# Hybrid attention block on one core: GpSimd forms the weight sums of gates and up stage, and gates' blocks take four groups of eight by seven products

## The chip, the cores and the metric

The kernel runs on one core of a Trainium2 chip. A core has five engines that each work through a queue of their own, in order: TensorE (PE: matmuls into PSUM, with a separate unit that loads weights), VectorE (DVE), ScalarE (ACT), GpSimd (POOL) and SyncE (SP, which here issues nearly all DMAs). They meet through semaphores. Operands lie in SBUF, 128 partitions wide; sums of matmuls in eight banks of PSUM. The metric is device time in microseconds (us) from the first to the last instruction, median of several runs.

## What is computed

One layer of a hybrid block on 256 tokens of width 2048, float32 throughout (the heads' attention is left out here):

```python
h = rms_norm(x, g_mix)
proj = h @ w_in                      # heads' queries, keys, values, and 3 x 2048 gate columns
o_fox, o_sb, o_mem = ...
g = sigmoid(gates.reshape(b, s, 3, 2048) + b_gate)
merged = g[:, :, 0] * (o_fox @ w_br_fox) + g[:, :, 1] * (o_sb @ w_br_sb) + g[:, :, 2] * (o_mem @ w_br_mem)
x = x + merged @ w_out
h2 = rms_norm(x, g_ffn)
u = causal_depthwise_conv(h2 @ w_up, conv_w, conv_b)     # w_up is 2048 x 11264
u_gate, u_val = split(u, 2)
x = x + (silu(u_gate) * u_val) @ w_down                  # w_down is 5632 x 2048
```

The weights are read once, so the kernel streams them: some 390 MB pass through the DMA queues in a run.

## The kernel before

**Split products.** TensorE reads float32 operands in a rounded form, so every weight tile of 128 x 1024 (`raw`) is split in two: ScalarE copies it rounded (`hi`, L143 in `piece`, L378 in `parts`), VectorE subtracts (`lo`, L144 and L379: two SBUF operands). A product is three matmuls (L384 to L386 in `three`): the two parts of the activations with `hi`, the first with `lo`. There are four buffers each for raw, hi and lo. In the up stage the same is done with two matmuls per tile (L1318, L1319).

**Seven products for eight.** In the functions that `blocked` drives, a group of two 128-row slices of weights (a "pair") times two halves of the tokens, on two halves of 1024 columns, is eight products of 512 columns: `eight`, written "e" in a plan. By a Strassen-Winograd scheme the same pair takes seven, "s", if four sums of the weights' quarters (T1 to T4) and four of the activations' quarters (formed by `pair_sums`) are there. The sums of activations for gates are the tile `xs`, one entry per "s" of a block, made in the background by `x_sums`, `GS` of them.

Where the weight sums come from differs:
- For `w_out` and `w_down` they are formed ahead, in stages that have time for it, and stored in HBM (`kept`). `sums_in` (L252 to L256) makes them with three VectorE adds on a staged tile of 128 x 1024 `pre` or `staged`: one of half its columns with a broadcast operand, two of a quarter each, where the tile is a half (`half_sums`); with a whole pair of 2048 columns (`pair_sums_ahead`) 1024, 512 and 512 columns. Both generators are stepped by `tick`, once per weight tile: they issue the load on SP, some ticks later the adds, some ticks later the store on SP. `half_sums` runs beside gates' plain block and the branch products, one half in 8 ticks; `pair_sums_ahead` runs in the stage of heads and again in the up stage, one pair in 8 ticks, from tick `DU` = 22 on, 17 pairs there.
- Two pairs of `w_down` get their sums in HBM itself (`sums_in_hbm`, L323): a tiny GpSimd copy that waits for an activation, then eight DMAs issued by GpSimd, four of them accumulating, each waiting for the one before it. `last_sums` starts the first at tick 148 of the up stage.
- For gates (`w_in`) the sums are formed on the spot: `prepared` (L492) loads the pair's two raw tiles and forms T1, T3, T2, T4 in two block tiles `t_g` with four VectorE adds of 512 columns (L496 to L499). It is called one pair ahead, and `seven_here` then splits and multiplies.

**Stages.** Memory keys and values, x, projections of the heads with their attention beside them (until about 304 us), gates and branches (304 to 655), `w_out` (to about 738), up (to 1226), down (to the end). Gates are six blocks of 1024 columns: the first is done plainly by `product`, five by `blocked` with a plan of eight letters, here "esesesee": two in a row, branch products, then three in a row, and branch products. In a block of gates, background generators are not stepped (`go_on`).

**Order.** A planner orders each engine's queue by the cost it expects of each instruction and by what is ready; `in_order` (`keep_in_program_order`) pins an instruction behind the one that was traced before it on its engine. The adds of `sums_in`, the loads and stores of the generators and the matmuls in `three` (from gates on) are pinned, the four adds of `prepared` are not.

**GpSimd** otherwise does little: masks of 128 x 128 in the heads' attention (L952, L983) and the DMAs of a few small rearrangements.

Of the kernel before, what the change touches and what calls it, by code (L numbers as in the profile page):

```python
# [10 lines left out]
F32 = mybir.dt.float32  # L11
F32R = mybir.dt.float32r
AF = mybir.ActivationFunctionType
ALU = mybir.AluOpType
AX = mybir.AxisListType

P = 128
# [17 lines left out]
WBUFS = 4  # L35
SBUFS = 4
BLOCKS = 14
GS = 3
PF = (6, 5)
DU = 22  # L40

# [2 lines left out]
def hybrid_block(  # L44
# [25 lines left out]
    nc = tc.nc  # L70
# [154 lines left out]


    o_plans = ("eessssse", "eessssse")
    g_plans = (("", "esesesee", "esesesee"), ("esesesee", "esesesee", "esesesee"))
    d_plans = (
        "efefefef" + "sef" * 4 + "ssefsfssfssee",  # L230
        "efsss" * 3 + "efssfsssssee",
# [2 lines left out]
    T1, T3, T4, T2 = range(4)  # L234
    FS2, FS4, FS3, FS1 = range(4)
    in_order = tc.keep_in_program_order
# [12 lines left out]
        for h in range(2)  # L249
    )  # L250

    def sums_in(w):  # L252
        both = w[:, 1:2].to_broadcast([P, 2, w.shape[2]])
        in_order(nc.vector.tensor_tensor(w[:, 0:2], w[:, 0:4:3], both, ALU.add))
        in_order(nc.vector.tensor_tensor(w[:, T2], w[:, T1], w[:, T2], ALU.add))
        in_order(nc.vector.tensor_tensor(w[:, T4], w[:, T2], w[:, T4], ALU.add))  # L256

    def kept_for(name, nb, pr):
        if (name, nb, pr) not in sums_of:
            at = f"kept_{name}{nb}_{pr}"  # L260
            sums_of[name, nb, pr] = dram.tile([P, 4, 512], F32, tag=at, name=at)
        return sums_of[name, nb, pr]

    def half_sums(staging, period, add, store, end):

        while halves and end not in issued:
            name, wv, nb, pr, h = halves.popleft()
            kept = kept_for(name, nb, pr)
            w = staging(f"pre_{name}{nb}_{pr}_{h}").rearrange("p (i c) -> p i c", i=4)
            n0 = nb * PIECE + h * 256  # L270
            for n in range(2):
                in_order(
                    nc.sync.dma_start(
                        w.rearrange("p (k n) c -> p k n c", k=2)[:, :, n],
                        wv[:, 2 * pr : 2 * pr + 2, n0 + n * 512 : n0 + n * 512 + 256],
                    )
                )
            for _ in range(add):
                yield
            sums_in(w)  # L280
            for _ in range(store - add):
                yield
            in_order(nc.sync.dma_start(kept[:, :, h * 256 : (h + 1) * 256], w))
            for _ in range(period - store):
                yield

    def pair_sums_ahead(staging, period, add, store, most=99, delay=0):

        due = deque()
        clock = 0  # L290
        for _ in range(delay):
            yield

        def step():
            while due and due[0][0] <= clock:
                _, kept, w = due.popleft()
                in_order(nc.sync.dma_start(kept, w))

        periods = cycle(period if isinstance(period, tuple) else (period,))
        while len(halves) > 1 and halves[0][-1] == 0 and most:  # L300
            most -= 1
            name, wv, nb, pr, _ = halves.popleft()
            halves.popleft()
            kept = kept_for(name, nb, pr)
            w = staging(f"pre_{name}{nb}_{pr}")
            in_order(
                nc.sync.dma_start(
                    w.rearrange("p (k c) -> p k c", k=2), wv[:, 2 * pr : 2 * pr + 2, nb * PIECE : (nb + 1) * PIECE]
                )
            )  # L310
            w = w.rearrange("p (i c) -> p i c", i=4)
            due.append((clock + store, kept, w))
            for t in range(next(periods)):
                if t == add:
                    sums_in(w)
                step()
                clock += 1
                yield
        while due:
            step()  # L320
            clock += 1
            yield
# [65 lines left out]
    def pair_sums(pair, w, groups):  # L388

        v = pair.bitcast(F32).rearrange("p k (l c) -> p k l c", l=2)  # L390
        wa, wr = w if isinstance(w, tuple) else (w[:, :512], w[:, 512:])
        a, r = (half.rearrange("p (i q) -> p i q", i=4) for half in (wa, wr))
        nc.vector.tensor_tensor(wa.rearrange("p (k c) -> p k c", k=2), v[:, :, 0], v[:, :, 1], ALU.add)

        a10 = a[:, 1:2].to_broadcast([P, 2, P])
        nc.vector.tensor_tensor(r[:, FS3 : FS1 + 1], a[:, 0:4:3], a10, ALU.subtract)
        nc.vector.scalar_tensor_tensor(r[:, FS2], r[:, FS1], -1.0, a[:, 0], ALU.mult, ALU.subtract)
        nc.vector.tensor_tensor(r[:, FS4], r[:, FS2], a[:, 2], ALU.add)
        for dst, which in groups:
            nc.scalar.copy(dst[..., 0, :], r[:, which])  # L400
        for dst, which in groups:
            nc.vector.tensor_tensor(dst[..., 1, :], r[:, which], dst[..., 0, :].bitcast(F32), ALU.subtract)
# [20 lines left out]
    def blocked(name, w, nb, n0, plan, pair, sums, raw_tile, t4_tile, gathered, ready=None, form=None, apart=None):  # L423
# [14 lines left out]
        def load(k):  # L438
            raw = raw_tile(f"raw_{name}{nb}_{k}")
            nc.sync.dma_start(raw, wv[:, k, n0 : n0 + PIECE])  # L440
            return raw
# [50 lines left out]
        def prepared(p):  # L492
            raw0, raw1 = load(2 * p), load(2 * p + 1)
            t13, t42 = (t4_tile(f"t{i}_{name}{nb}_{p}") for i in range(2))
            b0, b1, u, v = (w.rearrange("p (n c) -> p n c", n=2) for w in (raw0, raw1, t13, t42))
            nc.vector.tensor_tensor(u[:, 0], b0[:, 0], b0[:, 1], ALU.add)  # L496
            nc.vector.tensor_tensor(u[:, 1], b0[:, 1], b1[:, 1], ALU.add)
            nc.vector.tensor_tensor(v[:, 1], u[:, 0], b1[:, 1], ALU.add)
            nc.vector.tensor_tensor(v[:, 0], v[:, 1], b1[:, 0], ALU.add)  # L499
            return raw0, raw1, t13, t42  # L500

        def seven_here(p, first, last):
# [20 lines left out]
        for i, c in enumerate(plan):  # L523
            if c == "s":
                if s == 0:
                    if ready:
                        ready()
                    Y += [bank(f"y{name}{nb}_{j}") for j in range(4)]
                by_seven(sp[s], s == 0, s == ns - 1)
                s += 1  # L530
                if s == ns:
                    later(gathered(n0, Y))
            elif c == "f":
                form()
            else:
                eight(ep[e], i == 0, i == len(plan) - 1)
                e += 1
            if name == "g" and plan[i + 1 : i + 2] == "s":
                ahead[s] = prepared(s)
# [98 lines left out]
    def junk(name):  # L638
        return sm.tile([P, 512], F32, tag="junk", bufs=2, name=name)
# [25 lines left out]
    gp = mix.enter_context(tc.tile_pool(name="gp", bufs=3))  # L665
# [77 lines left out]
    w = {}  # L743
# [104 lines left out]
    def in_turn(name):  # L848
        turn[0] += 1
        return staged[:, turn[0] % 2]  # L850

    background.append(pair_sums_ahead(in_turn, PF, 3, 7, most=14))
    qm = heads_of(block("qm"))
    y = norm_heads(ps, rstd, "mq")
# [183 lines left out]
    background.clear()  # L1038
    xs = cst.tile([P, GS, 4, 2, P], F32R, tag="xres", name="xs")

    def x_sums():
        for _ in range(4):
            yield
        for p in range(GS):
            pair_sums(xT.pair(p), (junk(f"xa_{p}"), junk(f"xr_{p}")), [(xs[:, p], slice(0, 4))])
# [2 lines left out]

    background.append(x_sums())
    background.append(  # L1050
        half_sums(lambda name: gp.tile([P, 1024], F32, tag="pre", bufs=1, name=name), 8, 2, 5, "merged")
    )


# [150 lines left out]
    for nb, plan in enumerate(o_plans):  # L1205
# [18 lines left out]
    ends = []  # L1224
    ends_tile = lambda name, dt: ff.tile([P, 2, PIECE], dt, tag="ends", bufs=1, name=name)
    background.append(
        pair_sums_ahead(lambda name: ends_tile(name, F32).rearrange("p i c -> p (i c)"), 8, 1, 5, delay=DU)
    )
    a_done = []
    background.append(last_sums(148, 12))  # L1230
# [72 lines left out]
    for f0 in range(0, FT, 4):  # L1303
# [5 lines left out]
        for s in range(2):  # L1309
            ps = [bank(f"u{f0 + i}_{s}") for i in range(4)]  # L1310
            c0 = s * D_FF + f0 * P
            for k in range(0, KT, 2):
                hi, lo = piece(upv[:, k : k + 2, c0 : c0 + 512], 2, 512, f"u{f0}_{s}_{k}")
                for j in range(2):
                    first, last = k + j == 0, k + j == KT - 1
                    for i in range(4):
                        c = slice(i * P, (i + 1) * P)
# [63 lines left out]
    for nb, plan in enumerate(d_plans):  # L1381
# [5 lines left out]
        for t in range(NT):  # L1387
            for n in range(2):
                c = nb * PIECE + n * 512
                o = xres[:, t, c : c + 512]  # L1390
                nc.vector.tensor_tensor(o, o, X[t][n], ALU.add)
                if (nb, t, n) == (1, 1, 1):
                    nc.scalar.dma_start(ov[:, t, c : c + 256], o[:, :256])
                    c, o = c + 256, o[:, 256:]
# [35 lines left out]
```

## Time and profile before

| | |
|---|---|
| Median of 3 runs | 1457.82 us (1457.29 to 1458.19) |
| The profiled execution, span | 1457.8 us |
| TensorE busy | 1451.5 us |
| VectorE busy | 1229.2 us |
| ScalarE busy | 857.5 us |
| GpSimd busy | 33.0 us |
| DMA, mean over the span | 270 GB/s |

In the profile, "PE" is TensorE, "DVE" VectorE, "ACT" ScalarE, "POOL" GpSimd, "SPq" the queue of SyncE. A row of a timeline shows start, length, engine, line of the kernel, operation, output<-inputs, shapes, and in brackets how long the engine was idle before and what ended it. A row of grouped instructions ends in count, busy time, mean ns of one, and idle time before them. Matmuls are pipelined and their records overlap, so the distance of starts says more than their length; this holds for VectorE's records too, by less.

### The profile page before, as it was taken

What the parts mean: (1) busy time and instruction counts of PE and PEld (TensorE: products, weight loads), DVE (VectorE), ACT (ScalarE), POOL (GpSimd) and SP (SyncE); (2) the same over time, 40 slices, a digit from 0 to 9 for tenths busy, and PEclk for the clock granted to TensorE, in tenths of its full rate; (3) what the DMA queues carried; (4) which work ended last, traced back from release to release, by engine and by line L of the source; (5) the groups of instructions that cost most, each with busy time, mean ns of one, the idle gap of its engine ahead of it and who ended that gap; (6) DMA issues with size and microseconds to landing.
All of it is one profiled execution on the core that took longest, in us unless ns stands there. A gap on an engine that the chain in (4) does not pass through costs nothing.

```text
span 1457.8 us, 20647 instructions
## 1 busy us (share of the span) xinstructions
PE 1451.5 (100%) x7289; PEld 1227.1 (84%) x7289; DVE 1229.2 (84%) x1824; ACT 857.5 (59%) x1222; POOL 33.0 (2%) x70
## 2 busy tenths in 40 slices
PE   9999999999999999999999999999999999999998
PEld 7888888888888888888888888888888888888887
DVE  5788778776898899998987988888888877999988
ACT  6755445464554555546776656556556556676775
POOL 0000011010000000000000000000000010000000
PEclk9999999999999999999999999999999999999999
DMA  8797899777668576788877888888888899789996
GB/s 296 227 350 245 324 324 328 266 247 221 206 201 272 181 219 207 264 271 254 302 226 221 294 274 300 282 276 295 284 280 291 275 260 255 253 288 341 326 334 236
DMA packets 169415, 393.41 MB, mean 270 GB/s; under 512 B 12907, under 2 KB 30207, under 8 KB 165087
## 3 DMA queue, kind: packets, MB, share of 16 engines
q1 hardware_dynamic: 165822, 384.87, 79.3%
q0 software_dynamic: 2160, 5.12, 1.8%
q10 hardware_dynamic: 1328, 2.11, 0.4%
q8 instruction: 57, 0.93, 0.2%
q14 instruction: 48, 0.39, 0.1%
HBM read 353.24 MB, written 43.00 MB: 272 GB/s over the span
## 4 chain that ended last, share of the span: by engine, by line
PE 95%; DVE 1%; issue 1%; DMA 1%; POOL 0%; ACT 0%; DVEq 0%; POOLq 0%; ACTq 0%
PE u L1318 22%; PE u L1319 11%; PE xd L386 3%; PE xd L384 3%; PE xd L385 3%; PE xg L386 3%; PE xg L384 3%; PE xg L385 3%; PE s L386 2%; PE s L384 2%; PE f L384 2%; PE f L385 2%; PE f L386 2%; PE b L386 2%; PE s L385 2%; PE b L384 2%
## 5 line engine op out<-in xcount | busy, mean ns | idle before, releaser
L1318 PE MATMUL u<-hT,hi_u 128*128 128x512 f32 x1232 | 428.4, 394 | 0.0
L1319 PE MATMUL u<-hT,lo_u 128*128 128x256 f32 x1232 | 341.3, 277 | 0.0
L144 DVE TENSOR_TENSOR lo_u<-raw_u,hi_u 128x1024 fp32r<-128x1024 f32 x176 | 215.4, 1225 | 72.4 <-ACT hi_u L143 72.3
L1318 PEld LDWEIGHTS u<-hT,hi_u 128*128 128x128 f32 x1232 | 231.0, 188 | 53.5
L143 ACT CAST hi_u<-raw_u 128x1024 fp32r<-128x1024 f32 x176 | 184.7, 1050 | 130.1 <-PE u L1318 95.5
L1319 PEld LDWEIGHTS u<-hT,lo_u 128*128 128x128 f32 x1232 | 231.3, 188 | 0.0
L379 DVE TENSOR_TENSOR lo_d<-raw_d,hi_d 128x1024 fp32r<-128x1024 f32 x88 | 106.9, 1223 | 13.2 <-ACT hi_d L378 11.1
L378 ACT CAST hi_d<-raw_d 128x1024 fp32r<-128x1024 f32 x88 | 91.8, 1054 | 36.7 <-PE xd L385 11.9
L378 ACT CAST hi_g<-raw_g 128x1024 fp32r<-128x1024 f32 (+1 forms) x80 | 77.1, 972 | 49.8 <-PE xg L385 17.0
L379 DVE TENSOR_TENSOR lo_g<-raw_g,hi_g 128x1024 fp32r<-128x1024 f32 (+1 forms) x80 | 88.8, 1122 | 4.1 <-ACT hi_g L378 4.1
L384 PE MATMUL xg<-hi_g,xT 128*128 128x512 f32 x175 | 68.1, 389 | 0.0
L386 PE MATMUL xg<-lo_g,xT 128*128 128x512 f32 x175 | 68.1, 389 | 0.0
L385 PE MATMUL xg<-hi_g,xT 128*128 128x512 f32 x175 | 68.1, 389 | 0.0
L143 ACT CAST hi_f<-raw_f 128x1024 fp32r<-128x1024 f32 (+1 forms) x40 | 38.6, 968 | 46.4 <-PE f L385 29.9
L1318 PE MATMUL u<-hT_rest,hi_u 128*128 128x512 f32 x176 | 62.0, 394 | 0.0
L1268 ACT ACTIVATE y<-u,taps 128x256 f32<-128x256 f32 x88 | 49.6, 596 | 19.0 <-DVE u L1263 18.9
L144 DVE TENSOR_TENSOR lo_s<-raw_s,hi_s 128x1024 fp32r<-128x1024 f32 (+1 forms) x40 | 44.7, 1124 | 18.5 <-ACT hi_s L143 18.5
L143 ACT CAST hi_b<-raw_b 128x1024 fp32r<-128x1024 f32 x32 | 33.7, 1053 | 45.0 <-PE b L385 21.1
L144 DVE TENSOR_TENSOR lo_f<-raw_f,hi_f 128x1024 fp32r<-128x1024 f32 (+1 forms) x40 | 44.4, 1118 | 17.1 <-ACT hi_f L143 16.9
L143 ACT CAST hi_s<-raw_s 128x1024 fp32r<-128x1024 f32 (+1 forms) x40 | 38.2, 960 | 34.3 <-PE s L385 18.8
L378 ACT CAST hi_t_d<-raw_t_d 128x1024 fp32r<-128x1024 f32 (+1 forms) x54 | 43.5, 835 | 18.7 <-PE xd L385 11.6
L378 ACT CAST hi_t_g<-t_g 128x1024 fp32r<-128x1024 f32 x30 | 31.5, 1051 | 38.9 <-PE xg L385 35.6
(555 smaller groups left out, 3552.4 us busy)
## 6 DMA issues: line engine op xcount, KB each, us to landing
raw_u<-in_w_up_dram SPq DMA_DIRECT2D x176, 512.0 KB, 5.0
raw_g<-in_w_in_dram SPq DMA_DIRECT2D x96, 512.0 KB, 4.6
raw_d<-in_w_down_dram SPq DMA_DIRECT2D x61, 512.0 KB, 5.5
pre_d<-in_w_down_dram SPq DMA_DIRECT2D x17, 1024.0 KB, 7.8
kept_d<-pre_d SPq DMA_DIRECT2D x17, 1024.0 KB, 6.5
raw_f<-in_w_in_dram SPq DMA_DIRECT2D x32, 512.0 KB, 5.7
raw_s<-in_w_in_dram SPq DMA_DIRECT2D x32, 512.0 KB, 5.8
raw_t_d<-kept_d SPq DMA_DIRECT2D x27, 512.0 KB, 5.8
```

The source lines that it names most:

```text
L143: pin(nc.scalar.copy(hi[:, :m], raw[:, :m]))
L144: pin(nc.vector.tensor_tensor(lo[:, :m], raw[:, :m], hi[:, :m].bitcast(F32), ALU.subtract))
L378: nc.scalar.copy(hi[:, :n], src)
L379: nc.vector.tensor_tensor(lo[:, :n], src, hi[:, :n].bitcast(F32), ALU.subtract)
L384: fix(nc.tensor.matmul(o, lhsT=ah, rhs=w[0], start=first, stop=False))
L385: fix(nc.tensor.matmul(o, lhsT=al, rhs=w[0], start=False, stop=False))
L386: fix(nc.tensor.matmul(o, lhsT=ah, rhs=w[1], start=False, stop=last))
L1268: nc.scalar.activation(y, u[:, 2:], AF.Identity, scale=tap(2), bias=tap(3))
L1318: nc.tensor.matmul(ps[i], lhsT=hi[:, j, c], rhs=hT(k + j), start=first, stop=False)
L1319: nc.tensor.matmul(ps[i][:, :S], lhsT=lo[:, j, c], rhs=hT(k + j)[:, :S], start=False, stop=last)
```

## The change

Three things. The adds of `prepared` go from VectorE to GpSimd and are pinned in program order. `sums_in` gets an engine as a parameter; `half_sums` (beside gates) and the `pair_sums_ahead` of the up stage pass GpSimd, while that of the heads' stage, and `first_sums`, stay on VectorE. `GS` goes from 3 to 4, and the plan of gates' five blocks from "esesesee" to "essesese".

```diff
-GS = 3
+GS = 4
...
-    g_plans = (("", "esesesee", "esesesee"), ("esesesee", "esesesee", "esesesee"))
+    g_plans = (("", "essesese", "essesese"), ("essesese", "essesese", "essesese"))
...
-    def sums_in(w):
+    def sums_in(w, engine=None):
+        engine = engine or nc.vector
         both = w[:, 1:2].to_broadcast([P, 2, w.shape[2]])
-        in_order(nc.vector.tensor_tensor(w[:, 0:2], w[:, 0:4:3], both, ALU.add))
-        in_order(nc.vector.tensor_tensor(w[:, T2], w[:, T1], w[:, T2], ALU.add))
-        in_order(nc.vector.tensor_tensor(w[:, T4], w[:, T2], w[:, T4], ALU.add))
+        in_order(engine.tensor_tensor(w[:, 0:2], w[:, 0:4:3], both, ALU.add))
+        in_order(engine.tensor_tensor(w[:, T2], w[:, T1], w[:, T2], ALU.add))
+        in_order(engine.tensor_tensor(w[:, T4], w[:, T2], w[:, T4], ALU.add))
...
-            nc.vector.tensor_tensor(u[:, 0], b0[:, 0], b0[:, 1], ALU.add)
-            nc.vector.tensor_tensor(u[:, 1], b0[:, 1], b1[:, 1], ALU.add)
-            nc.vector.tensor_tensor(v[:, 1], u[:, 0], b1[:, 1], ALU.add)
-            nc.vector.tensor_tensor(v[:, 0], v[:, 1], b1[:, 0], ALU.add)
+            in_order(nc.gpsimd.tensor_tensor(u[:, 0], b0[:, 0], b0[:, 1], ALU.add))
+            in_order(nc.gpsimd.tensor_tensor(u[:, 1], b0[:, 1], b1[:, 1], ALU.add))
+            in_order(nc.gpsimd.tensor_tensor(v[:, 1], u[:, 0], b1[:, 1], ALU.add))
+            in_order(nc.gpsimd.tensor_tensor(v[:, 0], v[:, 1], b1[:, 0], ALU.add))
...
-        half_sums(lambda name: gp.tile([P, 1024], F32, tag="pre", bufs=1, name=name), 8, 2, 5, "merged")
+        half_sums(lambda name: gp.tile([P, 1024], F32, tag="pre", bufs=1, name=name), 8, 2, 5, "merged", nc.gpsimd)
...
-        pair_sums_ahead(lambda name: ends_tile(name, F32).rearrange("p i c -> p (i c)"), 8, 1, 5, delay=DU)
+        pair_sums_ahead(lambda name: ends_tile(name, F32).rearrange("p i c -> p (i c)"), 8, 1, 5, delay=DU, engine=nc.gpsimd)
```

(`half_sums` and `pair_sums_ahead` take the parameter and hand it to `sums_in`.)

More of the change, by code (lines that the diff above doesn't have):

```diff
@@ L262, in kept_for, with half_sums @@
         return sums_of[name, nb, pr]
-    def half_sums(staging, period, add, store, end):
+    def half_sums(staging, period, add, store, end, engine=None):
         while halves and end not in issued:
@@ L279, in half_sums @@
                 yield
-            sums_in(w)
+            sums_in(w, engine)
             for _ in range(store - add):
@@ L285, in half_sums, with pair_sums_ahead @@
                 yield
-    def pair_sums_ahead(staging, period, add, store, most=99, delay=0):
+    def pair_sums_ahead(staging, period, add, store, most=99, delay=0, engine=None):
         due = deque()
@@ L314, in pair_sums_ahead @@
                 if t == add:
-                    sums_in(w)
+                    sums_in(w, engine)
                 step()
```

## The prediction

> **What bounds the kernel now.** I read the page first, then the chain of waits, then the busy time by stretches, then the timeline of one gate block.
>
> ```profile
> span 1457.8 us, 20647 instructions
> ...
> PE 1451.5 (100%) x7289; PEld 1227.1 (84%) x7289; DVE 1229.2 (84%) x1824; ACT 857.5 (59%) x1222; POOL 33.0 (2%) x70
> ...
> PE 95%; DVE 1%; issue 1%; DMA 1%; POOL 0%; ACT 0%; DVEq 0%; POOLq 0%; ACTq 0%
> ```
>
> TensorE is the bound, with 95% of the chain. The profiled execution's span, 1457.8 us, is the median of the runs (1457.82), so sums start from 1457.8. Work taken from VectorE (DVE) gains only where DVE makes TensorE wait; a matmul taken away gains at once. The stretches show how much room DVE has:
>
> ```profile
> 304.00:351.00 47.00, 47.00 (x244) 40.32 (x243) 34.69 (x52) 27.63 (x43) 3.81 (x12) 1.00 0.85 275
> ...
> 380.00:438.00 58.00, 57.58 (x253) 46.98 (x252) 54.02 (x64) 32.81 (x35) 0.00 (x0) 1.00 0.67 209
> ...
> 524.00:618.00 94.00, 94.00 (x416) 77.54 (x415) 87.87 (x107) 53.56 (x57) 0.00 (x0) 1.00 0.72 230
> ...
> 800.00:1160.00 360.00, 360.00 (x2078) 314.82 (x2078) 313.36 (x513) 212.83 (x326) 1.10 (x2) 1.00 0.85 285
> ```
>
> Columns: stretch, length, then busy time of PE, PEld, DVE, ACT, POOL, granted clock, DMA. The first is gates' plain block, the second and third blocks with products by seven, the last most of the up stage. In the blocks by seven DVE is busy 93% (54.02 of 58, 87.87 of 94); in the up stage 87%. The granted clock is 1.00 throughout.
>
> **The gain on TensorE.** Three starts in the first block: a pair by eight, a pair by seven, the next pair.
>
> ```profile
> 360.88 0.39 PE L384 MATMUL xg<-hi_g,xT 128*128 128x512 f32 x1
> ...
> 366.32 0.39 PE L384 MATMUL yg<-hi_g,xT 128*128 128x512 f32 x1
> ...
> 371.08 0.39 PE L384 MATMUL xg<-hi_g,xT 128*128 128x512 f32 x1
> ```
>
> Eight products (24 matmuls) take 5.44 us, seven (21) 4.76 us. Turning one pair saves 0.68 us in each of the five blocks: **3.4 us, and nothing else shortens TensorE's work**. A block needs 3 x 4.76 + 5 x 5.44 = 41.5 us before, 4 x 4.76 + 4 x 5.44 = 40.8 after. The fourth xs group is five DVE passes no wider than 512 columns (under 5 x 0.69 = 3.5 us by the rows below) and one copy, inside the plain block, where DVE has 47 - 34.7 = 12.3 us idle: nothing.
>
> **The change on DVE's side in gates.**
>
> ```profile
> 424.90 0.69 DVE L497 TENSOR_TENSOR t_g<-raw_g,raw_g 128x512 f32<-128x512 f32 x1
> 425.50 0.69 DVE L498 TENSOR_TENSOR t_g<-t_g,raw_g 128x512 f32<-128x512 f32 x1
> 426.10 0.69 DVE L379 TENSOR_TENSOR lo_g<-raw_g,hi_g 128x512 fp32r<-128x512 f32 x1
> 426.70 0.69 DVE L499 TENSOR_TENSOR t_g<-t_g,raw_g 128x512 f32<-128x512 f32 x1
> 427.30 1.23 DVE L379 TENSOR_TENSOR lo_g<-raw_g,hi_g 128x1024 fp32r<-128x1024 f32 x1
> 428.44 1.23 DVE L379 TENSOR_TENSOR lo_t_g<-t_g,hi_t_g 128x1024 fp32r<-128x1024 f32 x1
> ```
>
> Records overlap; the starts say what a pass costs in a queue: 0.60 us for 512 columns, 1.14 for 1024. A pair by seven splits 512 + 3 x 1024 columns (4.0 us), by eight 2 x 1024 (2.3): the new pair adds 1.7 us. Leaving are 3 x 4 sums of 0.60, 7.2 us. Before, DVE had 93.5% of 41.5 = 38.8 us per block (third stretch); after, 38.8 - 7.2 + 1.7 = **33.3 us, 7.5 us of room under TensorE's 40.8**. If GpSimd's sixteen sums cost DVE nothing, the gate blocks are TensorE's alone.
>
> They do cost DVE. GpSimd (POOL) reads SBUF in this kernel already, in small mask passes:
>
> ```profile
> L983 POOL TENSOR_SCALAR_AFFINE_SELECT sb<-sb x24: 287/292/1277, 285.4 to 336.9; 128x128 f32<-128x128 f32 x24
> ...
> 228.75 1.22 DVE L254 TENSOR_TENSOR staged<-staged 128x1024 f32<-128x1024 f32 x1
> 228.91 1.22 POOL L952 TENSOR_SCALAR_AFFINE_SELECT fx<-fx 128x128 f32<-128x128 f32 x1 [7.72 <-DVE fx L951]
> ...
> 239.27 0.29 POOL L952 TENSOR_SCALAR_AFFINE_SELECT fx<-fx 128x128 f32<-128x128 f32 x1 [0.21 <-DVE fx L951]
> ...
> 239.30 1.33 DVE L144 TENSOR_TENSOR lo_s<-raw_s,hi_s 128x1024 fp32r<-128x1024 f32 x1
> ```
>
> The same 0.29 us mask takes 1.22 when a DVE add with two SBUF operands is running (it ends 0.16 after the add), and a DVE split that starts 0.03 us behind a mask takes 1.33 instead of 1.22. So the two engines exclude one another: POOL waits for the DVE pass, and DVE waits about 0.11 us for 128 columns with one operand. Most DVE passes of gates are of that kind (L379, two SBUF operands).
>
> What one POOL sum of 512 columns takes from DVE is the unknown. The mask row gives 0.11 / 128 = 0.86 ns a column and operand: two operands, 512 columns, 0.88 us. With the 0.03 us the split began later, 1.1 ns gives 1.1 us. From below, if the second operand is free: 0.45 us. From above, a whole instruction is held:
>
> ```profile
> L585 POOL TENSOR_SCALAR_AFFINE_SELECT after_r<-ones_r 128x128 fp32r<-128x128 f32 x1 | 0.3, 283 | 0.0
> ...
> L1416 POOL MEMSET const-float32-1.0<- 128x1 f32 x1 | 0.1, 98 | 0.0
> ```
>
> (283 - 98) / 128 = 1.45 ns a column, doubled and with 98 ns of start 1.58 us. I take 0.95 us, beside the first number; 0.45 and 1.58 stay for the range. Sixteen sums: 15.2 us against 7.5 of room.
>
> [...]
>
> What runs beside POOL at no cost are passes with a PSUM operand, an assumption from the kind of operand:
>
> ```profile
> L1134 DVE SCALAR_TENSOR_TENSOR g<-xg,scales,g 128x512 f32<-128x512 f32 x20 | 14.1, 746 | 0.0
> ...
> ACT hi_t_g L378 <- PE xg L385: 35.6, 24, 1.8
> ...
> 353.78 1.23 DVE L379 TENSOR_TENSOR lo_g<-raw_g,hi_g 128x1024 fp32r<-128x1024 f32 x1 [1.50 <-ACT hi_g L378]
> ```
>
> Four of L1134 a block, 14.1 / 5 = 2.8 us (bounds 0 and twice that, as gathering has as many more). The second row is the new wait: ScalarE's hi_t_g now waits for POOL. Until now it waited for TensorE to free a buffer, 35.6 / 24 = 1.5 us each, which is the cover. Two POOL sums of 1.15 us (0.95 and some start-up), each behind a DVE pass of 1.14, are 4.6 us against 1.2 on DVE: 3.4 later, 1.9 uncovered, 7.6 a block at most; queued behind that copy are the next pair's hi_g copies, their DVE splits and TensorE. As POOL works while DVE idles, I count 1.5 of these 7.6. The block is then 33.3 + 15.2 - 2.8 + 1.5 = **47.2 us, 5.7 more than 41.5**. Five make 28.5. The third row takes some back: entering the blocks DVE is ahead; the first block's split starts at 353.78, ends near 355.0 and is used after 360.88, 6 us of lead. Two blocks run in a row, then three after the branch products, so 6 us are absorbed twice: 28.5 - 12 = **16.5 us**. DMAs are the same in number and size; raws are held until POOL has read them, which is inside the 7.6.
>
> **The up stage.** Seventeen sums of 1024 + 512 + 512 columns move:
>
> ```profile
> L254 DVE TENSOR_TENSOR pre_d<-pre_d 128x1024 f32<-128x1024 f32 x17 | 20.7, 1220 | 0.0
> ...
> 1138.68 0.34 SPq L297 DMA_DIRECT2D kept_d<-pre_d  x1
> ...
> 1146.16 0.37 SPq L307 DMA_DIRECT2D pre_d<-in_w_down_dram  x1
> ...
> 1146.62 14.56 SPq L142 DMA_DIRECT2D raw_u<-in_w_up_dram  x6
> ...
> 1161.42 0.34 SPq L297 DMA_DIRECT2D kept_d<-pre_d  x1
> ...
> 1158.70 0.55 POOL L335 DMA_DIRECT2D kept_d<-in_w_down_dram  x1
> ...
> 1189.03 0.82 POOL L336 DMA_DIRECT2D kept_d<-in_w_down_dram  x1 [8.12 <-DMA kept_d<-in_w_down_dram]
> ```
>
> On DVE they cost 17 x (1.14 + 2 x 0.60) = 40 us of 313; on POOL, at 0.95 per 512 columns, 17 x 3.8 = 65. DVE's 313 - 40 + 65 = 338 stays under 360, so no wait on average (at 1.58 it is 381: 21 too many; at 0.45, 304). Convolutions bunch DVE's work at the start of every group, so I count 2 us. The six half sums beside gates' plain block and branch products are hidden by the idle DVE there.
>
> One place is special. The last sum's turn comes three ticks after the first of the sums made in HBM, and POOL keeps order: it stands behind eight DMA issues that run from 1158.70 to 1189.03. Its store (the row at 1161.42) is on SP, with raw_u loads behind it. Held there for 31 us, less the three to four ticks of 2.8 us that buffers cover, TensorE would lose some 20 to 25 us. Six loads precede that store where program order has five, so the planner moves loads ahead of a store that isn't ready; I count 0.
>
> **Sum:** 1457.8 + 16.5 + 2 = **1476**, slower.
>
> **Rivals.**
> - Faster, DVE not held: the place is the gate blocks, the price POOL's hold on DVE, and the point at which it decides is a hold of (7.5 + 2.8) / 16 = 0.64 us per 512 columns. Below it TensorE bounds the blocks: 1457.8 - 3.4 = **1454.4**. For it: the 0.45 us bound and DVE's 7.5 us of room. Against: two operands have to be read.
> - Near that point: a hold of 0.6 to 0.75, a little over or under, lead absorbing what is over: 1455.5 to 1460.5, say **1457**.
> - The last up-stage sum is stuck behind POOL's DMAs as well: 1476 + 25 = **1501**. For it: POOL's order and the 31 us; against: the planner's hoisting.
> - That the change doesn't do what it says: xs for four groups has just the size of the tile it shares, and POOL takes such adds; I give this no share.
>
> **How the numbers follow.** Forecast 0.52, DVE not held 0.20, near the point 0.15, last sum stuck 0.13. About 0.2% (2.9 us) is what a measurement of this kernel can tell from no change: faster 0.20, same 0.15, slower 0.65. The gain is bounded by 3.4 us, so the range starts at 1453.5; a hold of 1.58 gives 16 x 0.63 x 5 = 50 us more than 1476, which I cut at 1512, some 0.1 lying above. The forecast's own range is 1462 to 1512.
>
> **What would show it.** Right: DVE's L379 records stretched beyond 1.23 us beside POOL; POOL sums of 512 columns lasting over 1 us; TensorE waiting for lo_t_g or t_g in the gate blocks, which last 45 us or more. Wrong: L379 unchanged, blocks of 40.8 us. A gap of 10 us or more on TensorE near 1180 would show the last sum stuck.

## The result and the profile after

The changed kernel takes **1501.21 us** (median of four runs, 1496.26 to 1504.80) against 1458.01 for the kernel before: 1.0293 times as long (95% interval 1.0268 to 1.0319). Forecast was 1476. The profiled execution is 1503.1 us long, 45.3 more than that of before; its page:

```profile
span 1503.1 us, 20725 instructions
...
PE 1467.6 (98%) x7274; PEld 1231.4 (82%) x7274; DVE 1290.9 (86%) x1710; ACT 861.6 (57%) x1233; POOL 312.0 (21%) x219
...
PE 88%; DVE 5%; DMA 3%; issue 2%; POOL 1%; ACT 1%; SPq 0%; DVEq 0%; ACTq 0%; POOLq 0%
```

VectorE has 114 instructions fewer than before (1710 for 1824) and is busy 62 us longer (1290.9 for 1229.2); GpSimd went from 33 to 312 us. VectorE was given less work and takes longer over it. In the chain of work that ended last TensorE has 88%, not 95%.

Where the 45.3 us lie comes from stage lengths: in the timeline of TensorE, the start of the first matmul of a stage to that of the next. At the first matmul of `w_out`, in the groups of before and of after:

```profile
L384 PE MATMUL xo<-hi_o,mT x58: 389/389/481, 659.5 to 741.8; 128*128 128x512 f32 x58
```

```profile
L385 PE MATMUL xo<-hi_o,mT x58: 389/389/481, 683.4 to 765.7; 128*128 128x512 f32 x58
```

(Shortest, middle and longest of the group in ns, first and last start in us; line numbers of after are one higher here.) `w_out` starts 23.9 us later and takes as long as before. All stages, in us:

| stage | before | after | difference |
|---|---|---|---|
| up to the first gate matmul | 309.4 | 310.0 | +0.6 |
| gates and branches | 350.1 | 373.4 | +23.3 |
| `w_out` | 83.0 | 83.0 | 0 |
| up | 490.0 | 511.0 | +21.0 |
| down, to the end | 225.4 | 225.7 | +0.3 |

So there are two losses of about one size, in the two places where GpSimd took over sums. First the gates. Two stretches of blocks by seven, of before and of after (stretch, length, then busy time of PE, PEld, DVE, ACT, POOL, granted clock, DMA share, GB/s):

```profile
360.90:444.90 84.00, 83.58 (x367) 68.53 (x366) 74.69 (x89) 49.12 (x51) 0.00 (x0) 1.00 0.66 212
482.00:622.00 140.00, 140.00 (x622) 115.77 (x621) 128.57 (x159) 77.48 (x83) 0.00 (x0) 1.00 0.68 218
```

```profile
363.10:452.70 89.60, 84.93 (x361) 67.75 (x361) 85.78 (x63) 52.22 (x55) 57.35 (x33) 0.98 0.65 192
489.00:640.00 151.00, 140.99 (x599) 113.88 (x599) 148.68 (x115) 78.22 (x84) 91.20 (x51) 0.97 0.62 190
...
1200.00:1240.00 40.00, 29.31 (x156) 24.75 (x155) 16.97 (x29) 13.98 (x23) 11.83 (x14) 0.87 0.78 196
```

VectorE fills 148.68 of 151 us (98%) with fewer instructions, 115 for 159: it has become the bound there, and TensorE waits for it. The last row is the second place, near the end of the up stage, where TensorE is busy 29 of 40 us. TensorE's waits say the same (awaited, releaser: us in total, times, longest), the longest in the gates of before first, then after:

```profile
PE xg L386 <- DVE lo_t_g L379: 0.3, 1, 0.3
```

```profile
PE xg L387 <- DVE lo_g L380: 11.4, 4, 3.7
...
PE u L1319 <- ACT hi_u L143: 10.2, 1, 10.2
...
PE g L385 <- DVE sb L1016: 1.6, 1, 1.6
```

In after the first is VectorE's split in the gate blocks, the second one single gap in the up stage, the third lies in the plain block (taken up further below). All waits of TensorE in blocks and branches come to 16.1 us; some 9 us more are matmuls that run slower behind a wait (the granted clock of 0.98 and 0.97 in the rows above; last section). And this is how a VectorE pass and a GpSimd sum take turns, first VectorE's timeline, then GpSimd's in the same stretch, then both groups over all of gates:

```profile
560.28 8.49 DVE L380 TENSOR_TENSOR lo_g<-raw_g,hi_g 128x1024 fp32r<-128x1024 f32 x4
```

```profile
559.26 2.26 POOL L497 TENSOR_TENSOR t_g<-raw_g 128x512 f32<-128x512 f32 x1 [6.69 <-DMA raw_g<-in_w_in_dram]
561.48 2.28 POOL L498 TENSOR_TENSOR t_g<-raw_g,raw_g 128x512 f32<-128x512 f32 x1
563.72 2.27 POOL L499 TENSOR_TENSOR t_g<-t_g,raw_g 128x512 f32<-128x512 f32 x1
566.07 1.62 POOL L500 TENSOR_TENSOR t_g<-t_g,raw_g 128x512 f32<-128x512 f32 x1
```

```profile
L380 DVE TENSOR_TENSOR lo_g<-raw_g,hi_g x80: 675/1781/2328, 357.4 to 631.6; 128x1024 fp32r<-128x1024 f32 x60, 128x512 fp32r<-128x512 f32 x20
...
L497 POOL TENSOR_TENSOR t_g<-raw_g x20: 1291/1750/2348, 358.8 to 619.0; 128x512 f32<-128x512 f32 x20
```

Four splits that took 1.14 us each before take 8.49 together, while four sums run beside them in 8.4. The longest split is 2.328 us, a free one is 1.22 to 1.23 (the prediction's rows): a sum of 512 columns **holds VectorE for 1.10 us**, where the forecast took 0.95. The shortest sum of that group lasts 1.29, so nearly all of it, 1.10 of 1.29 us, is exclusive. Passes of VectorE with an operand in PSUM weren't held, as the prediction assumed: eleven of them (L1135, 128x512) ran under a sum of GpSimd in after and lasted 0.736 to 0.742 us, no longer than in before (0.746 on average).

### The profile page after: what moved, and what is told of

Same layout as the page of the kernel before. It is cut to its first block, busy times and chain, and to the rows that moved or that the text cites. A ratio compares the mean times of both kernels' runs of the same rounds, so it can differ in the third digit from the quotient of the medians.

```text
span 1503.1 us, 20725 instructions
## 1 busy us (share of the span) xinstructions
PE 1467.6 (98%) x7274; PEld 1231.4 (82%) x7274; DVE 1290.9 (86%) x1710; ACT 861.6 (57%) x1233; POOL 312.0 (21%) x219
## 4 chain that ended last, share of the span: by engine, by line
PE 88%; DVE 5%; DMA 3%; issue 2%; POOL 1%; ACT 1%; SPq 0%; DVEq 0%; ACTq 0%; POOLq 0%
PE u L1319 20%; PE u L1320 10%; PE xd L385 3%; PE xd L387 3%; PE xd L386 3%; PE xg L387 2%; PE s L387 2%; PE xg L385 2%; PE s L385 2%; PE f L385 2%; PE f L386 2%; PE f L387 2%; PE s L386 2%; PE xg L386 2%; DVE lo_g L380 2%
## 5 line engine op out<-in xcount | busy, mean ns | idle before, releaser
L1319 PE MATMUL u<-hT,hi_u 128*128 128x512 f32 x1232 | 437.2, 399 | 10.2 <-ACT hi_u L143 10.2
L1320 PE MATMUL u<-hT,lo_u 128*128 128x256 f32 x1232 | 346.3, 281 | 0.5 <-DVE lo_u L144 0.5
L144 DVE TENSOR_TENSOR lo_u<-raw_u,hi_u 128x1024 fp32r<-128x1024 f32 x176 | 248.9, 1428 | 69.4 <-ACT hi_u L143 66.3
L380 DVE TENSOR_TENSOR lo_g<-raw_g,hi_g 128x1024 fp32r<-128x1024 f32 (+1 forms) x80 | 138.3, 1762 | 2.4 <-ACT hi_g L379 2.1
L255 POOL TENSOR_TENSOR pre_d<-pre_d 128x1024 f32<-128x1024 f32 (+1 forms) x23 | 56.8, 2468 | 317.9 <-DMA pre_d<-in_w_down_dram 299.9
L379 ACT CAST hi_t_g<-t_g 128x1024 fp32r<-128x1024 f32 x40 | 42.0, 1051 | 57.9 <-PE xg L386 37.7
L387 PE MATMUL xg<-lo_g,xT 128*128 128x512 f32 x140 | 55.6, 397 | 11.7 <-DVE lo_g L380 11.4
L380 DVE TENSOR_TENSOR lo_t_g<-t_g,hi_t_g 128x1024 fp32r<-128x1024 f32 x40 | 54.4, 1385 | 5.7 <-ACT hi_t_g L379 5.6
L385 PE MATMUL xg<-hi_g,xT 128*128 128x512 f32 x140 | 54.9, 392 | 1.6 <-DVE g L1135 1.6
```

Of the source, the lines that this page charges most:

```text
L144: pin(nc.vector.tensor_tensor(lo[:, :m], raw[:, :m], hi[:, :m].bitcast(F32), ALU.subtract))
L255: in_order(engine.tensor_tensor(w[:, 0:2], w[:, 0:4:3], both, ALU.add))
L379: nc.scalar.copy(hi[:, :n], src)
L380: nc.vector.tensor_tensor(lo[:, :n], src, hi[:, :n].bitcast(F32), ALU.subtract)
L385: fix(nc.tensor.matmul(o, lhsT=ah, rhs=w[0], start=first, stop=False))
L387: fix(nc.tensor.matmul(o, lhsT=ah, rhs=w[1], start=False, stop=last))
```

## The experiments

Two theories for gates: the **hold** (it fills VectorE; the expectations call this theory "ports", and no run shows what makes the hold), and **lateness** (the sums reach ScalarE later because GpSimd is slow, and the copy behind them is late). Two for the up stage: the **last store** is stuck behind GpSimd's DMA issues, or the hold costs there too. Times are medians, ratios stand against the kernel before in the same launch (medians 1458.0 to 1458.9); stage lengths come from the profiled execution of each kernel, to about 0.1 us.

| kernel | median us | ratio and interval | gates | up |
|---|---|---|---|---|
| before | 1458.0 | 1 | 350.1 | 490.0 |
| after | 1501.2 | 1.0293 (1.0268 to 1.0319) | 373.4 | 511.0 |
| reads on GpSimd added to before | 1504.1 | 1.0308 (1.0293 to 1.0324) | 396.4 | 490.0 |
| late sums that read nothing | 1457.9 | 0.9999 (0.9990 to 1.0008) | 350.2 | 489.9 |
| sums with one operand | 1459.6 | 1.0003 (0.9994 to 1.0012) | 351.3 | 489.9 |
| gates' part alone | 1483.8 | 1.0173 (1.0158 to 1.0188) | 373.7 | 489.9 |
| four groups, all on VectorE | 1470.4 | 1.0081 (1.0066 to 1.0096) | 361.3 | 489.9 |
| three groups, gates on GpSimd | 1463.7 | 1.0037 (1.0024 to 1.0051) | 355.9 | 489.9 |
| four groups in first blocks only | 1463.9 | 1.0036 (1.0023 to 1.0048) | 355.3 | 490.0 |
| after, sums in HBM four ticks later | 1488.9 | 1.0204 (1.0178 to 1.0231) | 375.7 | 498.1 |
| up stage's part alone | 1473.8 | 1.0121 (1.0092 to 1.0149) | 348.6 | 503.5 |
| up stage's part, four ticks later | 1460.7 | 1.0024 (1.0011 to 1.0037) | 349.4 | 499.0 |
| fills in place of up's sums | 1458.8 | 1.0008 (0.9997 to 1.0019) | 348.8 | 489.9 |

### Hold or lateness

**Reads beside the kernel before.** In each pair by seven GpSimd adds four times what nobody uses, from `xs` into a tile nobody reads; VectorE still makes the sums, so they can't be late by GpSimd's pace. The copy of one column lets the adds start when VectorE's first sum is there.

```diff
+            in_order(nc.gpsimd.tensor_copy(j[:, :1], u[:, 0, :1]))
+            for _ in range(4):
+                in_order(nc.gpsimd.tensor_tensor(j, x0, x1, ALU.add))
```

> The kernel before (three groups, sums on VectorE), with four adds more on GpSimd in every call of prepared, 512 columns each, from xs into a tile that nobody reads, started when VectorE's first sum is there. [...] Theory (ports): each add holds VectorE for 1.1 us, the excess of the longest stretched split in the changed kernel (2328 - 1224 ns): a block asks 38.8 + 12 x 1.1 - some 5 beside PSUM passes and waits = 47 us against 41.5, so gates become 20 to 30 us longer: 1478 to 1488. Rival (GpSimd's sums are late, the chain is longer): 1458 to 1460.

Gates grew by **46.3 us**, 0.77 per added sum (60 of them), by far the most of all kernels and well over the 20 to 30 us expected; the groups, and TensorE's longest wait:

```profile
L379 DVE TENSOR_TENSOR lo_g<-raw_g,hi_g x80: 679/1216/2325, 353.0 to 653.0; 128x1024 fp32r<-128x1024 f32 x65, 128x512 fp32r<-128x512 f32 x15
...
L502 POOL COPY beside_g<-t_g x15: 185/1176/4662, 360.4 to 632.4; 128x1 f32<-128x1 f32 x15
```

```profile
PE xg L386 <- DVE lo_g L379: 16.3, 13, 3.7
```

The longest split has the same length as in after, 2325 ns. VectorE had 41.5 - 38.8 = 2.7 us of room in each of five blocks (the prediction's figures), 13.5 in all: (46.3 + 13.5) / 60 = 1.0 us per sum, if VectorE alone sets the length. VectorE's own records there, each against the middle length of its like in before, are 50.5 us longer in all, **0.84 us per sum**; in the rest is TensorE's slower pace behind its waits (matmuls of `xg` last up to 632 ns, the middle one 389, and the granted clock of the execution is 0.994). So adds on GpSimd make the loss without anything being late by them; that it is their reading, and not their writing, shows in the next kernel.

**Late sums that read nothing.** Gates' part alone, each sum left out and replaced by a copy of one column and two fills of 511 columns. GpSimd takes about as long (1.66 us in place of a sum, 1.81 in after, on average) and the copies behind it wait for it.

```diff
-            in_order(nc.gpsimd.tensor_tensor(u[:, 0], b0[:, 0], b0[:, 1], ALU.add))
...
+            for dst, raw in ((u[:, 0], b0), (u[:, 1], b1), (v[:, 1], b1), (v[:, 0], b1)):
+                in_order(nc.gpsimd.tensor_copy(dst[:, :1], raw[:, 0, :1]))
+                in_order(nc.gpsimd.memset(dst[:, 1:], 0.5))
+                in_order(nc.gpsimd.memset(dst[:, 1:], 0.5))
```

> Four groups, up stage on VectorE (as in the run with gates only), but the four GpSimd adds of prepared are replaced by a copy of one column of the raw tile and two fills of 511 columns each, some 1.1 us together: the sums are left out, GpSimd is as late as an add of 1.29 us, almost, and reads next to nothing. Theory (ports): the hold goes, VectorE has 33.3 us of a block's 40.8, gates take 347 to 351 us and the time is 1454.5 to 1459. Rival (lateness): within 5 us of the run with gates only, 1479 to 1484.

```profile
ACT hi_t_g L379 <- POOL t_g L500: 8.4, 5, 2.4
...
PE g L385 <- DVE sb L1016: 2.2, 1, 2.2
```

ScalarE does wait for GpSimd, five times, 8.4 us in all (in after three times, 6.4 us), and the time is that of before: 1457.94, gates 350.2. VectorE's records are 2.6 us longer in all, and 71.0 in after. **Lateness of this size costs nothing; the hold costs all of it.** The pins in program order are in this kernel too, so they cost nothing either. The second row is a loss that remains, in the plain block, with the half sums still on GpSimd: that block takes 55.9 us and not 51.5, by 2.5 us of waits and some 2 us of slower matmuls behind them. Blocks and branches take 294.3 us against 298.6, so TensorE's 3.4 us showed in full.

**One operand.** The sums are left out; in their place stand copies of 512 columns on GpSimd.

```diff
-            in_order(nc.gpsimd.tensor_tensor(u[:, 0], b0[:, 0], b0[:, 1], ALU.add))
...
+            in_order(nc.gpsimd.tensor_copy(u[:, 0], b0[:, 0]))
```

> Four groups, up stage on VectorE (as in the run with gates only), with each of the four GpSimd adds of prepared replaced by a copy of 512 columns of the raw tile: the sums are left out, GpSimd reads one operand instead of two. If the hold goes by operands read: the longest stretched split is 1224 + 550 = 1775 ns, a block asks 33.3 + 16 x 0.55 = 42.1 us of VectorE, as much as with four groups on VectorE (42.9), so gates near 360 us, time 1466 to 1470. If it goes by the instruction, whatever it reads: split up to 2330 ns, gates near 373 us. If a copy doesn't hold VectorE: 1458, as with fills.

```profile
L380 DVE TENSOR_TENSOR lo_g<-raw_g,hi_g x80: 675/1216/1840, 358.0 to 609.5; 128x1024 fp32r<-128x1024 f32 x60, 128x512 fp32r<-128x512 f32 x20
...
L499 POOL COPY t_g<-raw_g x20: 603/1064/1612, 362.4 to 599.3; 128x512 f32<-128x512 f32 x20
```

The longest split is 1.840 us, so a copy holds 1.840 - 1.224 = 0.62 us, about its whole shortest length (0.603). Gates are 351.3, and 350.1 before, so next to nothing: the hold came out near the 0.55 expected, the 360 us of gates didn't. The expectation took the longest hold for the mean. VectorE's records in blocks and branches are 16.1 us longer in all, under 0.2 us for each of 80 copies, where after has 71.0 for 80 sums (three half sums are in both). The room that the prediction worked out is 7.5 us in each of five blocks, 37.5: the copies' 16.1 fit into it, the sums' 71.0 don't. The loss isn't in proportion to the hold, it starts where VectorE's room ends.

### The fourth group, and who makes the sums

**Gates' part alone** (up stage back on VectorE):

```diff
-        pair_sums_ahead(..., 8, 1, 5, delay=DU, engine=nc.gpsimd)
+        pair_sums_ahead(..., 8, 1, 5, delay=DU)
```

> The changed kernel with the up stage's sums back on VectorE. Gates' loss alone: the trace of the changed kernel has 23.3 us more from the first gate matmul to the first of w_out, so 1480 to 1483. TensorE's pace in the up stage: 0.347 us a pair of matmuls as before if GpSimd's adds there set it to 0.353, 0.353 in some executions if it is a state of its own.

Gates take 373.7, as in after, and the up stage 489.9, as in before: the two losses are apart, and gates' is 25 us of the time (1483.81).

**Four groups, all sums on VectorE:** `GS` and plan of after, every `nc.gpsimd` of the sums back to `nc.vector`.

> Four groups by seven, all sums on VectorE as before. By the working of the prediction a block asks 33.3 + 16 x 0.60 = 42.9 us of VectorE and 40.8 of TensorE, against 38.8 and 41.5 before: 1.4 us more a block, less what a lead of 6 us absorbs twice: 1454 to 1462. If TensorE's saved 3.4 us come through: 1454.5. If GpSimd was needed for four groups: over 1462.

It was 1470.4 and not 1454 to 1462. A window over three blocks, and TensorE's waits:

```profile
484.00:630.00 146.00, 140.04 (x612) 113.15 (x611) 137.77 (x171) 80.56 (x87) 0.00 (x0) 1.00 0.67 207
```

```profile
PE xg L387 <- DVE lo_g L380: 5.4, 7, 0.8
```

VectorE at 94% makes TensorE wait already, in pieces of at most 0.8 us. The prediction's own figures give 38.8 + 1.7 of splits + 4 x 0.60 of sums = 42.9 us of VectorE per block, 1.4 more than the 41.5 that a block took before, so 7.0 in five. Measured are +11.2: +9.9 in blocks and branches, 2.0 a block, and +1.3 in the plain block, where TensorE now waits 1.0 us for the heads' `sb`, so the fourth `xs` group, which the prediction priced at nothing, isn't quite free there. So **the fourth group loses without GpSimd too**: before, with 93% on VectorE, was at the edge.

**Three groups, gates' sums on GpSimd** (on gates' part alone, so the up stage's sums are on VectorE):

```diff
-GS = 4
+GS = 3
-    g_plans = (("", "essesese", "essesese"), ("essesese", "essesese", "essesese"))
+    g_plans = (("", "esesesee", "esesesee"), ("esesesee", "esesesee", "esesesee"))
```

> Gates' sums and the half sums on GpSimd with three groups by seven as before, up stage on VectorE. Theory (ports): a block asks 38.8 - 7.2 + 12 x 1.1 - 5 = 39.8 us of VectorE and 41.5 of TensorE, so little is lost: 1458 to 1464. If lateness or each GpSimd sum costs what it costs with four groups (23.6 / 80 = 0.3 us a sum): 60 x 0.3 = 18 us, 1476.

With that the four cases are complete (gates in us, as plain block + blocks and branches; the half sums are where gates' sums are):

| | sums on VectorE | sums on GpSimd |
|---|---|---|
| three groups | 350.1 (51.5 + 298.6) | 355.9 (55.6 + 300.3) |
| four groups | 361.3 (52.8 + 308.5) | 373.7 (53.3 + 320.4) |

In blocks and branches GpSimd loses 1.7 with three groups and 11.9 with four; the fourth group loses 9.9 or 20.1. Most of what GpSimd loses with three groups is in the plain block, where only the half sums are on it. By the four-group row a sum on GpSimd takes 11.9 / 80 = 0.15 us more than the 0.60 it took on VectorE, 0.75 net; VectorE's own records gave 0.84. Both are less than the hold of 1.10, since part of the sums falls beside passes it doesn't hold, or VectorE's idle time.

**Four groups in the first block of each row only**, on the kernel before: each row's first block has the lead of about 6 us on VectorE that the prediction let absorb the excess.

```diff
-GS = 3
-    g_plans = (("", "esesesee", "esesesee"), ("esesesee", "esesesee", "esesesee"))
+GS = 4
+    g_plans = (("", "essesese", "esesesee"), ("essesese", "esesesee", "esesesee"))
```

> The kernel before, all sums on VectorE, with four groups by seven only in the first block of each row of blocks, where VectorE enters ahead. If the lead of 6 us pays for the 4 us that a fourth group asks of VectorE there: 2 x 0.68 = 1.4 us less, 1457. If the lead is needed for the blocks behind: by the share of the run with four groups in all blocks (11.3 us for five), 2 x 2.3 = 4.5 us more, 1463.

Gates are 355.3, +5.1: +0.9 in the plain block and +4.2 for the two blocks, 2.1 each, as in the kernel with four groups in all blocks. **The lead absorbs nothing.** Why not, whether VectorE's own waits use it up or it isn't there to be spent, wasn't tried.

### The up stage

**The sums in HBM four ticks later**, on after: the mark that starts GpSimd's DMA issues then stands behind the last sum in GpSimd's queue.

```diff
-    background.append(last_sums(148, 12))
+    background.append(last_sums(152, 12))
```

> The changed kernel with the first of the sums made in HBM started at tick 152 of the up stage instead of 148, so that on GpSimd they stand behind the last up-stage sum and not ahead of it. Theory: the last sum, held behind eight DMA issues, held its store and with it SP's loads; TensorE's 10.2 us gap near 1222 us and the slow clock behind it (about 2 us) go, and the time falls by 10 to 13 us from the changed kernel's. Rival (the up stage loses because GpSimd's adds hold VectorE): the gap stays somewhere in the up stage and the time stays within 3 us.

The median fell by 12.3 us to 1488.9, the up stage by 12.9. Here is the place in after, on GpSimd (mark, first and last DMA issue, the sum), on SP and on TensorE:

```profile
1188.70 0.44 POOL L327 COPY mark_d<-aT 128x1 f32<-128x1 f32 x1 [18.30 <-ACT aT L177]
1189.08 0.55 POOL L336 DMA_DIRECT2D kept_d<-in_w_down_dram  x1
...
1215.57 0.82 POOL L337 DMA_DIRECT2D kept_d<-in_w_down_dram  x1 [5.68 <-DMA kept_d<-in_w_down_dram]
1216.14 2.67 POOL L255 TENSOR_TENSOR pre_d<-pre_d 128x1024 f32<-128x1024 f32 x1
```

```profile
1176.53 27.09 SPq L142 DMA_DIRECT2D raw_u<-in_w_up_dram  x10
1221.56 0.34 SPq L298 DMA_DIRECT2D kept_d<-pre_d  x1
1221.99 27.04 SPq L142 DMA_DIRECT2D raw_u<-in_w_up_dram  x11
```

```profile
1222.05 0.28 PE L1320 MATMUL u<-hT,lo_u 128*128 128x256 f32 x1
1232.56 0.79 PE L1319 MATMUL u<-hT,hi_u 128*128 128x512 f32 x1 [10.22 <-ACT hi_u L143]
...
1234.19 0.63 PE L1319 MATMUL u<-hT,hi_u 128*128 128x512 f32 x1
1234.83 0.63 PE L1319 MATMUL u<-hT,hi_u 128*128 128x512 f32 x1
```

The sum runs right behind the last DMA issue, which stands behind the mark, and that had waited 18.3 us for its activation; its store reaches SP at 1221.56; SP had been idle since 1176.53 + 27.09 = 1203.6 with the next eleven weight loads behind that store; TensorE runs dry and waits 10.2 us. In the kernel with the later mark, GpSimd and SP:

```profile
1182.50 2.59 POOL L255 TENSOR_TENSOR pre_d<-pre_d 128x1024 f32<-128x1024 f32 x1 [11.55 <-DMA pre_d<-in_w_down_dram]
...
1193.61 0.44 POOL L327 COPY mark_d<-aT 128x1 f32<-128x1 f32 x1 [5.66 <-ACT aT L177]
```

```profile
1193.26 0.43 SPq L298 DMA_DIRECT2D kept_d<-pre_d  x1
...
1195.79 19.20 SPq L142 DMA_DIRECT2D raw_u<-in_w_up_dram  x9
```

Sum before mark, and no gap. But the up stage is 498.1 there, 8.1 above before, with no wait of TensorE to show for it.

**The up stage's part alone**, on before: only `pair_sums_ahead` of the up stage gets `engine=nc.gpsimd`.

> The kernel before with the up stage's sums alone on GpSimd, gates untouched. If losses add: 1458 plus 12 us for the held store, plus up to 8 us for the slower pace: 1470 to 1479, with TensorE's one long gap near 1200 us. Rival (the changed kernel's loss is all gates', the gap belongs to it): 1458 to 1461.

1473.8; the held store again, and up at 503.5 in the profiled execution. One of the four executions took 1481.82, the others 1472 to 1474. **The same with the later mark** (`last_sums(152, 12)`):

> The kernel before with the up stage's sums on GpSimd and the sums made in HBM started at tick 152, gates untouched. Theory: without the held store the up stage has room for GpSimd's hold (VectorE busy 322 of 360 us in the run with the up stage only), so 1458 to 1459 in most executions; if the slower pace is tied to GpSimd's sums, some are 8 us longer. Rival (the hold costs the up stage too): 1460 or more in all.

1460.7 over twelve executions, of which nine lie between 1458.8 and 1462.0 (middle 1460.4) and three between 1467.4 and 1467.5; the profiled one is of the long kind. The nine are 1.6 us above before (1458.8), and only one lies in the 1458 to 1459 expected. So seventeen sums on GpSimd cost little here and not nothing: VectorE's records in the stage are 48.7 us longer, and TensorE's only wait in it is 0.6 us for a split (both in the profiled execution). **Fills in place of the sums**, to see whether reading makes the long kind:

```diff
-    def sums_in(w):
+    def sums_in(w, engine=None):
+        if engine is not None:
+            for part in (w[:, 0:2], w[:, 0:2], w[:, T2], w[:, T2], w[:, T4], w[:, T4]):
+                in_order(engine.memset(part, 0.5))
+            return
```

> The kernel before with the up stage's sums replaced by GpSimd fills (six a pair; the sums are left out), and the sums made in HBM started at tick 152. GpSimd writes as much as with sums and reads nothing. Up stage 490 us, 1458. If the slower pace of TensorE (0.353 us a pair for 0.347), seen only where GpSimd forms the up stage's sums, comes with GpSimd's activity as such: some of the executions 7 us longer; if with its reads: none.

1458.8: ten executions between 1457.9 and 1461.0, one 1467.58. So the long kind comes without reads as well (once in eleven against three in twelve, too few to say that it is rarer), and its cause stays open (last section).

None of these kernels is faster than the one before; that one remains the best.

## Why the prediction was right in direction and wrong in size

Direction and range held; the effect was +43 us and not +18.

- **The failed step: "I count 0"** for the last sum of the up stage. It cost 12.9 us of the up stage. The prediction saw the mechanism and the 31 us, and let the planner's moving loads ahead of the store decide. By SP's row ten loads stand ahead of that store where program order has five, so the planner did move some, and that wasn't enough: SP stood still for 18 us. It was less than the rival's 20 to 25, presumably because these loads covered more than three to four ticks. That the total falls on this rival's 1501 is chance: its store was too dear, its gates too cheap, and the slower pace wasn't in it.
- **"28.5 - 12 = 16.5"** for gates: measured +23.3. Two errors against each other. A block loses 4.3 us (23.3 less 1.6 for the plain block, by five) and not 5.7. The hold was mis-sized (up to 1.10, not 0.95), but what a sum took from VectorE on average, 0.75 to 0.84, is near the forecast's (16 x 0.95 - 2.8) / 16 = 0.78; the 1.5 us for lateness were too much (next point). And the lead of 6 us, taken off twice, doesn't exist in the measured time; that is the larger error, 12 us.
- **1.5 of 7.6 us for lateness**: measured nothing, by the late sums that read nothing.
- **The half sums beside the plain block, "hidden by the idle DVE there"**: not quite. TensorE waits 1.6 us there, and by the rows it is the held store once more, in small. (With three groups and the half sums on GpSimd the waits there are 2.1 us and with three groups on VectorE none; the fourth group alone gives 1.0, so how the 1.6 divide isn't shown.) In after, a half sum on GpSimd, then SP, then ScalarE:

```profile
326.32 2.26 POOL L255 TENSOR_TENSOR pre_d<-pre_d 128x512 f32<-128x512 f32 x1
...
329.67 1.60 POOL L257 TENSOR_TENSOR pre_d<-pre_d 128x256 f32<-128x256 f32 x1
```

```profile
323.53 0.34 SPq L478 DMA_DIRECT2D raw_t_o<-kept_o  x1
331.30 0.53 SPq L284 DMA_DIRECT2D kept_d<-pre_d  x1
331.93 1.34 SPq L142 DMA_DIRECT2D raw_g<-in_w_in_dram  x2
```

```profile
337.10 1.05 ACT L143 CAST hi_g<-raw_g 128x1024 fp32r<-128x1024 f32 x1 [5.77 <-DMA raw_g<-in_w_in_dram]
338.06 0.51 ACT L1017 ACTIVATE sb<-sb 128x384 f32<-128x384 f32 x1
```

  The half sum follows the heads' masks on GpSimd and is done at 331.27; its store, and behind it the loads of `raw_g`, stand on SP from 323.87 to 331.30; ScalarE waits 5.77 us for `raw_g` with the heads' `sb` in its queue behind that copy; and `sb` is what TensorE then waits for. Cover was looked for on VectorE's time and not along the result's way out.
- **"2 us" for the up stage's sums**: right in size, 1.6 in nine of twelve executions without the held store.
- **A further 8.1 us of the up stage** was foreseen by nothing: TensorE's slower pace, all of it by the figures of the last section.
- **TensorE's 3.4 us**: right where VectorE wasn't held: blocks and branches were 4.4 us shorter then, less about 1 us by which they vary from kernel to kernel with nothing changed in them. The rival "DVE not held" put its point of decision at a hold of 0.64, and nothing contradicts it: holds of 0.62 and none give 351.3 and 350.2, a hold of 1.10 gives 373.7. But the copies took under 0.2 us on average, so no run lies near that point.

The sum as measured, in the profiled execution: 0.6 + 23.3 + 12.9 + 8.1 + 0.3 = 45.2 of 45.3 us. Two of the four executions of after are, by their time, without the slow pace (1496.26 and 1497.93), which makes the median's +43.2.

## What to carry to other kernels

Moving an add of two SBUF operands to GpSimd relieves VectorE only if it holds VectorE for less time than it took there: here up to 1.10 us, and 0.75 to 0.84 on average, for 0.60, so VectorE got fewer instructions and more time. VectorE at 93% beside the bound had no room to give here; price an added pass at full length, and don't let a lead pay for it unless an experiment shows that it does. When compute moves into the queue of an engine that also issues DMAs waiting for each other, follow what its result releases: a store on another queue, and the loads behind that (it happened here for 12.9 us, and in small, for up to 1.6 us, in the plain block).

## What the runs showed of the hardware

**TensorE at a slower pace with the granted clock shown as 1.00.** The up stage repeats a pair of matmuls of 512 and 256 columns. Starts of the 512 in before, in after, and in the up stage's part with the later mark:

```profile
1099.68 0.40 PE L1318 MATMUL u<-hT,hi_u 128*128 128x512 f32 x1
...
1120.48 0.40 PE L1318 MATMUL u<-hT_rest,hi_u 128*128 128x512 f32 x1
```

```profile
1099.91 0.40 PE L1319 MATMUL u<-hT,hi_u 128*128 128x512 f32 x1
...
1120.76 0.40 PE L1319 MATMUL u<-hT,hi_u 128*128 128x512 f32 x1
```

```profile
1099.93 0.40 PE L1319 MATMUL u<-hT,hi_u 128*128 128x512 f32 x1
...
1120.78 0.40 PE L1319 MATMUL u<-hT,hi_u 128*128 128x512 f32 x1
```

Sixty pairs lie between the first two, 59 between the others: 20.80 / 60 = 0.3467 us, 20.85 / 59 = 0.3533. In after the slow pace holds from 829 us to the end of the stage at 1277, but for some 15 us around the gap: 1226 pairs, each 0.0067 us longer, 8.2 us. By the window of after from 766 to 1200 us nothing waits and the clock is full:

```profile
766.00:1200.00 434.00, 434.00 (x2470) 376.97 (x2469) 382.10 (x543) 252.81 (x397) 105.85 (x54) 1.00 0.80 270
```

Executions 7 to 8 us longer, as this would make them, came in 2 of 4 of after, 2 of 4 of the one with the later mark, 1 of 4 of the up stage's part alone, 3 of 12 of that with the later mark, 1 of 11 of the fills; in none of the 41 of the seven other kernels, which have no sums or fills of GpSimd in the up stage, nor in those of before. So the long executions came only with GpSimd busy in that stage. The pace itself doesn't need that: in before, too, the first pairs of the stage follow at 0.353 us (13 from 742.85 to 747.44), and at 0.347 from 749.4 on, behind eight small matmuls of another kind (L197). In the three profiled long executions it sets in at one point, at 829, 833 and 805 us, each time within 3.3 us of the end of a split that a GpSimd sum had stretched to 2.31 us, the last time right behind a wait of TensorE of 0.57 us. But equal stretches elsewhere, in the up stage's part alone above all, don't set it off. What decides is open.

**After a gap, TensorE restarts slowly.** After 10.2 us of idling the pairs follow at 0.64 us (1234.19 to 1234.83) in place of 0.353, until 1236.75, and the granted clock of that stretch of 40 us is 0.87. A gap costs more than its length, here some 2 us (0.5 of it a second wait, for `lo_u`). It is the same in small in gates: behind the waits of 3.6 to 3.7 us in after, and behind one wait of 1.8 to 2.5 us in the plain block of three kernels (late sums, one operand, three groups on GpSimd), some 5 to 13 matmuls of 512 columns start 0.427 us apart and not 0.227. Behind the waits of 1.6 and 1.7 us in the plain blocks of after and of gates' part alone they don't. The length of the wait doesn't decide alone: in the kernel with added reads one of 1.84 us isn't followed by it, and in the one with four groups in first blocks a pair of waits of 0.75 and 0.77 is.

**A small GpSimd instruction can wait long for VectorE.** The copy of one column above lasted 0.185 us when free and up to 4.662, with six two-operand passes of VectorE running back to back; no sum of 512 columns for gates lasted over 2.353 in after. What decides whose turn it is wasn't tried.
